# Sigmoid gates stored to DRAM ahead of the scan, and the last branch merge woven by 256 tokens into the output products

## The chip, the cores and the metric

The kernel runs on one core of a Trainium2 chip, as one program on one set of inputs. The metric is the device time of one execution in microseconds (us). The core has a matrix engine (TensorE, PE in the rows, with its weight loads as PEld), a vector engine (VectorE, DVE), a scalar engine (ScalarE, ACT), GpSimd (POOL) and SyncE (SP), which here only issues DMAs. Each engine takes its instructions in the order in which they were placed; an instruction that waits holds up all that stand behind it on that engine.

## The reference

One step of a backbone of one layer, for two groups of tokens: 2048 sample tokens and 128 prompt tokens, 2176 in all, with D = 1024 features.

```python
shift, scale, gate = ada_mod(c, w_ada, b_ada)          # silu(c) @ w_ada + b_ada
xn = rmsnorm(h, ln_g) * (1.0 + scale) + shift
proj = xn @ w_in
qkv, beta, dec, z_a, u_b, v_b, z_b, x_c, z_c, gates = split(proj)
qkv = silu(conv3(qkv))                                  # short centred convolution
o, s_f, s_b = delta_bidir(q, k, v, g, beta, s0_f, s0_b) # A: scan over chunks of 64 tokens, both directions
o_a = rmsnorm(o, o_norm_g) * silu(z_a)
o_b = chunk_sgu(u_b, v_b, ...) * silu(z_b)              # B: spatial gating in chunks of 128
o_c = fourier_mix(x_c, grid) * silu(z_c)                # C: Fourier mixing
pb = [o_a, o_b, o_c] @ w_branch                         # three products 512 -> 1024
merged = sum_n sigmoid(gates[n]) * pb[n]
h = h + gate * (merged @ w_out)
y = rmsnorm(h, final_g)                                 # the final scan states are outputs too
```

## The kernel before

Activations are kept turned (features on partitions) as a pair of fp16 tensors, `xh` and `xl` (high part and remainder, [128, 8, 2176] each). A product of two such pairs is three matmuls (high by high, low by high, high by low). All are recorded at one helper line, L250 (L249 in the changed kernel), so a row's tensors tell what it belongs to. Tokens go in four tiles of 512 and one of 128 (`TBS`).

Weights come by blocks of 128 output columns: `read_w` loads a block in fp32 into `wst` (two buffers), and `converting` makes the pair: ScalarE squares it (L315), a one-column matmul and VectorE make a scale, ScalarE writes the high part (L327), VectorE the low part (L328). `wlist` holds all blocks in the order of use, `getw` takes the next and reads some ahead, `weight_step` does a piece of a conversion between main work.

Main work goes through stages in this order: (1) adaLN, norm and silu(z_a), to 150 us; (2) qkv with its convolution and the decays, to 440; (3) branch B (V, then U and Z_b) and branch C (X_c and Z_c, Fourier steps); (4) `merge(1)`, `merge(2)`, `merge(0)`: per block of 128 output columns and per tile, a gate product of 24 matmuls, its sigmoid on ScalarE into `sg`, a branch product of 12 matmuls, VectorE's product of both (L1739, L1742), and for branches 2 and 0 POOL's sum with what the branches before left (L1743; `mrow`, loaded from and stored to the DRAM tensor `mrg`); (5) the output, `two_tiles` for 256 tokens at a time.

The branch operand is loaded from DRAM (`br`) by `branch_block` (L1689, into `st`, three buffers) and converted into `big` (ScalarE L1699, VectorE L1700). The output uses seven half-size products in place of eight: sums of quarters of w_out are made by `out_w` and staged in DRAM (`tw`), sums of the merged operand by `quarters` within `merge(0)`, staged in `pa`, and both are loaded again by the output. Sample rows for the residual go into `xh`, which nothing reads any more by then (`room`).

Beside stages 3 and 4 runs branch A's delta rule, a generator of small steps (`delta`): first 17 chunk preparations, then an inverse, then the scan of 33 steps and the finished rows. `Pace` interleaves it: each piece of main work adds its estimated microseconds, and for every `QUOTA` = 1.6 (preparation) or `SCAN` = 1.3 (scan) of them one step of the generator is recorded. So the amounts of main work set where on each engine the scan's instructions stand. Preparation lies from 440 to 800 us, the scan's first chain is at 915, its last at 1622. SP's queue carries nearly all loads, in the order of their places.

Of the kernel before, what the change touches and what calls it, by code (L numbers as in the profile page):

```python
# [20 lines left out]
P = 128  # L21
# [11 lines left out]
SCAN = 1.3  # L33
# [4 lines left out]
ADA_D = (6, 7, 12, 13, 14, 15)  # L38
TBS = [(0, 512), (512, 512), (1024, 512), (1536, 512), (2048, 128)]
# [72 lines left out]
def _blocks():  # L112


    parts = [(C_ZA, g) for g in range(4)] + [(C_QKV, i) for i in range(12)] + [(C_V, g) for g in range(4)]
    for pair in ((C_U, C_ZB), (C_XC, C_ZC)):
        parts += [(x_, g) for g in range(4) for x_ in pair]
    return parts + [(C_G + n * D, db) for n in (1, 2, 0) for db in range(KT)]
# [76 lines left out]
def hybrid_flow_kernel(ctx: ExitStack, tc: tile.TileContext, x_prompt, x_sample, state_delta, c, c_ctx, w_ada,  # L195
# [48 lines left out]
    newest, gated_, queued = [None], [None], [False]  # L244

    def behind_gate():
        return tc.issue_after(gated_[0].ins) if queued[0] else ExitStack()
# [37 lines left out]
    turn_of = [None]  # L285
# [10 lines left out]
    def read_w(src, nkt, cols=P, tag="w"):  # L296
        st = sb(wp, [P, nkt, cols], "wst" if cols == P else tag + "st", bufs=2 if cols == P else 1)
        load(st, src.rearrange("p (k c) -> p k c", c=cols))
        return st
# [3 lines left out]
    def converting(w, st, nkt, cols=P, hi=None, lo=None, tag="w", bufs=5, nth=0):  # L303
# [4 lines left out]
        if tag == "v":  # L308
            hi, lo = [t[:, vfilled[0]] for t in v4]
            vfilled[0] += 1  # L310
        w.hi = sb(wpool, [P, nkt, cols], tag + "hi", F16, bufs=bufs) if hi is None else hi
        w.lo = sb(wpool, [P, nkt, cols], tag + "lo", F16, bufs=bufs) if lo is None else lo
        ss = sb(wp, [P, 1], "wss", bufs=4) if nth < KT else bsums[:, 3 + nth:4 + nth]
        with behind_gate():
            w.squared = A.activation(w.lo, st, AF.Square, accum_out=ss)  # L315
# [6 lines left out]
        if isx is None:  # L322
            w.own = inv
        else:
            V.tensor_mul(w.inv, inv, isx)
# [34 lines left out]
    for i, (n_, g) in enumerate(_blocks()):  # L360
        wlist.append((w_blk[i], KT, "z" if n_ == C_ZA else "v" if n_ == C_V else "w", 4))
        if n_ >= C_G:
            n_ = (n_ - C_G) // D
            wlist.append((w_brb[n_, g], 4, "b", 2, n_ * KT + g))
    v4, vfilled = [], [0]
    goal = [0]
# [11 lines left out]
    def begin():  # L378

        i = len(wdone)  # L380
        if i >= goal[0] or (wlist[i][2] == "b" and not bwp):
            return False
# [3 lines left out]
        wsteps.append(converting(wdone[i], wread[i], wlist[i][1], tag=wlist[i][2], bufs=wlist[i][3], nth=(wlist[i] + (0,))[4]))  # L386
# [544 lines left out]
    for ct in range(12):  # L931
        w = getw(1, 2 if ct < 6 else min(4, 15 - ct))
# [24 lines left out]
    wsn = sb(ep, [P, WB], "st", bufs=3).rearrange("p (g q) -> p g q", g=4)  # L957
    with tc.issue_after(behind.ins):
        SY.dma_start(wsn, w_spatial[0].rearrange("g p q -> p g q"))
# [511 lines left out]

    vsD = dram("vs", [4, P, NTOK])
    bs = ExitStack()
# [33 lines left out]
    for t in range(NCH):  # L1507
        ps = bank(ps_mm, [P, 4, P])
        ts = slice(t * P, (t + 1) * P)
        for k in range(KT):  # L1510
            mm(ps, xh[:, k, ts], v4[0][:, :, k, :], k == 0, False)
            mm(ps, xh[:, k, ts], v4[1][:, :, k, :], False, False)
            mm(ps, xl[:, k, ts], v4[0][:, :, k, :], False, k == KT - 1)
        vn = sb(ep, [P, WB], "sg", bufs=4).rearrange("p (i c) -> p i c", i=4)
# [151 lines left out]
    cfs.close()  # L1666


    mD = dram("mrg", [KT, P, NTOK])
    HALVES = [(0, 1024, TBS[0:2]), (1024, 1152, TBS[2:])]  # L1670

    ms_ = ExitStack()
    bwp.append(pool(ms_, "bwp", 1))
    big = pool(ms_, "big", 1)
    mrp = pool(ms_, "mrp", 2)

    o16 = sb(big, [P, 2, 4, NTOK], "big", F16)

    def branch_scale(n, cols):
        ss = sb(ep, [P, 1], "bss2")  # L1680
        V.tensor_reduce(ss, oss[n][:, 0:cols], AX.X, ALU.add)
        V.tensor_copy(bsums[:, n:n + 1], ss)
        return scales(ss, ep, "bsc")

    def branch_block(n, s, t0, tn):

        def loaded(g):
            st = sb(ep, [P, tn], "st", bufs=3)
            SY.dma_start(st, obD[n][g, :, t0:t0 + tn])  # L1689
            return st  # L1690

        sts = [loaded(g) for g in range(3)]
        yield
        for g in range(4):
            if g == 1:
                sts.append(loaded(3))
            st = sts[g]
            with behind_gate():
                A.activation(o16[:, 0, g, t0:t0 + tn], st, AF.Copy, scale=s)  # L1699
            V.scalar_tensor_tensor(o16[:, 1, g, t0:t0 + tn], st, s, o16[:, 0, g, t0:t0 + tn], ALU.mult, ALU.subtract)  # L1700

    def merge(n, first, inv, each=None, halves=HALVES, mid=None, then=None, step=None):

        steps, sinv = iter(()), None
        for db in range(KT):
            gw, bw = getw(2, 2)
            binv = sb(ep, [P, 2], "binv")
            V.tensor_mul(binv[:, 0:1], inv, bw.inv)
            V.tensor_mul(binv[:, 1:2], binv[:, 0:1], sx)
            if each is not None:  # L1710
                each(db)
            if db == KT - 1 and then is not None:
                s_, sinv = branch_scale(*then)
            for h0, hn, tbs in halves:
                mrow = sb(mrp, [P, hn], "mrow")
                if not first:
                    SY.dma_start(mrow, mD[db][:, h0:h0 + hn])
                if each is not None and (n == 0 or db > 3):
                    next(gates, 0)
                for t0, tn in tbs:  # L1720
                    m4 = None
                    if n == 0 and db > 3 and tn == 512:
                        m4 = sb(ep, [P, tn], "st", bufs=3)
                        SY.dma_start(m4, mD[db - 4][:, t0:t0 + tn])
                    if first and db == 0:
                        for tb in TBS[0:2] if t0 == 0 else TBS[TBS.index((t0, tn)) + 1:][:1]:
                            for _ in branch_block(n, s1_, *tb):
                                pass
                    ps = bank(ps_mm, [P, tn])
                    gemm_T(ps, gw, 0, xh[:, :, t0:t0 + tn], xl[:, :, t0:t0 + tn])  # L1730
                    sg = sb(ep, [P, tn], "sg", bufs=4)
                    with tc.high_priority():
                        gated_[0] = A.activation(sg, ps, AF.Sigmoid, scale=gw.inv)  # L1733
                    ps = bank(ps_mm, [P, tn])
                    gemm_T(ps, bw, 0, o16[:, 0, :, t0:t0 + tn], o16[:, 1, :, t0:t0 + tn], nkt=4)
                    mr = mrow[:, t0 - h0:t0 - h0 + tn]
                    if first:
                        with tc.high_priority():
                            V.scalar_tensor_tensor(mr, ps, binv[:, 1:2], sg, ALU.mult, ALU.mult)  # L1739
                    else:  # L1740
                        with tc.high_priority():
                            V.scalar_tensor_tensor(sg, ps, binv[:, 1:2], sg, ALU.mult, ALU.mult)  # L1742
                        G.tensor_tensor(mr, mr, sg, ALU.add)  # L1743
                    if m4 is not None:
                        quarters(db - 4, t0, m4, mr)
                    if n == 0 and t0 == NS and db == KT - 1:
                        as_pair(p16[0][:, db, :], p16[1][:, db, :], mr, ms_s)
                    weight_step()
                    if step is not None:
                        step(db)  # L1750
                    pace.tick(tn * MT)
                    if sinv is not None:
                        for _ in steps:
                            pass
                        steps = branch_block(then[0], s_, t0, tn)
                        next(steps, 0)
                if n:
                    (SY if first else G).dma_start(mD[db][:, h0:h0 + hn], mrow)
                elif db < 4:
                    G.dma_start(mD[db][:, h0:h0 + hn], mrow)  # L1760
                elif h0 and db < KT - 1:
                    G.dma_start(mD[db][:, NS:NTOK], mrow[:, NS - h0:NTOK - h0])
                if mid is not None and db == KT - 1:
                    mid(h0)
        for _ in steps:
            pass
        return sinv

    gateD = dram("gate", [2, D])

    def gate_rows():
        for blk in range(4):
            cs = slice(2 * D + blk * 256, 2 * D + (blk + 1) * 256)
            acc = sb(ep, [P, 512], "sg", bufs=4).rearrange("p (g c) -> p g c", g=2)
            for k0 in range(0, KT, 4):
                st = sb(wp, [P, 4, 256], "wst", bufs=2)
                SY.dma_start(st, w_ada_[k0 * P:(k0 + 4) * P, cs].rearrange("(k p) c -> p k c", p=P))
                yield 1
                ada_sum(acc, st, range(k0, k0 + 4), k0 == 0)
                yield 1  # L1780
# [412 lines left out]
```

## Time and profile before

| | us |
|---|---|
| median of three runs | 2145.65 |
| the runs | 2145.1, 2145.65, 2146.66 |
| span of the profiled execution (first to last instruction) | 2142.8 |
| PE busy in it | 2084.4 |
| mean granted TensorE clock in it | 0.990 of full |

The profile is one execution on the chip. Its own time is known by its span alone; the median of the runs is 2.85 us above that. In rows of groups, `x64` is a count, then come busy us in total, mean ns of one, idle time of the engine before them and what ended it. In rows by window come the length, busy us and count for each engine, the granted clock, the share of the 16 DMA engines' time and GB/s.

### The profile page before, as it was taken

The page shows a single profiled execution, that of the slowest core. Times are in us where ns is not written, and L with a number is a line of the kernel's source. Part 1 is how long each engine was busy: PE and PEld are TensorE (multiplying, and loading weights), DVE is VectorE, ACT ScalarE, POOL GpSimd, SP SyncE. Part 2 cuts the span into 40 slices and gives each one's busy share as a digit, 9 for nine tenths or more (in the row PEclk, how much of TensorE's full clock was granted, in tenths as well). Part 3 has the DMA queues.
Part 4 walks back from the last instruction along what each step waited for, and adds up shares of the span by engine and source line. Part 5 has one row for each costly group of instructions (what it writes and reads, how often), then busy time and mean ns, then how long its engine had stood idle before and what let it go on. Part 6 is the DMA issues. An engine that isn't in the chain of part 4 may idle for free.

```text
span 2142.8 us, 42632 instructions
## 1 busy us (share of the span) xinstructions
PE 2084.4 (97%) x16133; PEld 1197.6 (56%) x16133; DVE 1330.7 (62%) x2945; ACT 1060.6 (49%) x2456; POOL 843.1 (39%) x1089
## 2 busy tenths in 40 slices
PE   8999999999999999999899999999999999999998
PEld 4454444455555677777555556565655444444443
DVE  6656854378777786566655555866665564666245
ACT  5554744465656664445544445665654353443112
POOL 0321332225565554552322233355543234343464
PEclk9999999999999999999999999999999999999999
DMA  9625722177877743444665556867664645456862
GB/s 352 222 78 191 266 103 103 62 222 234 262 226 240 228 143 99 121 132 141 204 182 166 164 160 188 262 211 226 211 198 128 210 169 173 167 197 234 344 221 89
DMA packets 222766, 403.25 MB, mean 188 GB/s; under 512 B 39704, under 2 KB 109616, under 8 KB 219744
## 3 DMA queue, kind: packets, MB, share of 16 engines
q1 hardware_dynamic: 167520, 290.58, 42.5%
q0 software_dynamic: 15216, 65.89, 8.2%
q10 hardware_dynamic: 39824, 44.05, 6.0%
q8 instruction: 127, 2.08, 0.4%
q14 instruction: 79, 0.65, 0.1%
HBM read 258.19 MB, written 142.24 MB: 187 GB/s over the span
## 4 chain that ended last, share of the span: by engine, by line
PE 50%; DVE 8%; DMA 7%; POOL 3%; ACT 3%; issue 3%; SPq 1%; ACTq 0%; POOLq 0%; DVEq 0%
PE b L250 49%; DMA st<-br 3%; POOL E L1115 1%; DMA pa<-pa 1%; DVE XB L1114 1%; POOL st L1466 1%; DVE big L1700 1%; DMA ei<-XB 1%; ACT big L1699 1%; ACT nd L1066 0%; DVE n L1083 0%; POOL ss L1024 0%; DVE XB L1123 0%; DMA br<-st 0%; DMA skn<-kv 0%
## 5 line engine op out<-in xcount | busy, mean ns | idle before, releaser
L250 PE MATMUL b<-xh,whi 128*128 128x512 f16 (+1 forms) x1920 | 650.3, 347 | 2.9 <-DVE sg L1456 1.8
L250 PE MATMUL b<-xl,whi 128*128 128x512 f16 (+1 forms) x1920 | 650.6, 347 | 0.0
L250 PE MATMUL b<-xh,wlo 128*128 128x512 f16 (+1 forms) x1920 | 649.7, 347 | 0.0
L250 PEld LDWEIGHTS <-whi 128*128 128x128 f16 x3856 | 352.4, 98 | 326.1 <-issue 6.9
L250 PEld LDWEIGHTS <-wlo 128*128 128x128 f16 x1928 | 188.6, 98 | 175.6 <-issue 1.2
L250 PE MATMUL b<-big,bhi 128*128 128x512 f16 (+1 forms) x960 | 253.2, 348 | 2.8 <-ACT big L1699 1.5
L250 PE MATMUL b<-big,blo 128*128 128x512 f16 (+1 forms) x480 | 163.4, 347 | 0.0
L1743 POOL TENSOR_TENSOR mrow<-mrow,sg 128x512 f32<-128x512 f32 (+1 forms) x80 | 94.4, 1183 | 129.4 <-DVE sg L1742 98.6
L953 POOL TENSOR_TENSOR cy<-cy,raw 128x545 f32<-128x545 f32 (+1 forms) x48 | 64.5, 1372 | 182.1 <-ACT raw L952 182.1
L250 PEld LDWEIGHTS <-xh 128*128 128x128 f16 x1496 | 117.1, 98 | 28.7 <-issue 1.3
L250 PEld LDWEIGHTS <-bhi 128*128 128x128 f16 x960 | 87.8, 98 | 79.2 <-issue 4.0
L1115 POOL TENSOR_TENSOR E<-E,XB 128x31 f32<-128x31 f32 (+15 forms) x155 | 94.3, 608 | 83.8 <-DVE XB L1114 67.6
L250 PEld LDWEIGHTS <-xl 128*128 128x128 f16 x1068 | 98.1, 98 | 44.8 <-DMA tw<-tw 1.3
L1733 ACT ACTIVATE sg<-b,winv 128x512 f32<-128x512 f32 (+1 forms) x120 | 74.0, 616 | 86.3 <-PE b L250 85.5
L1188 POOL COPY T<-ES 32x256 f16<-32x256 f16 x68 | 30.0, 442 | 182.9 <-DMA ES<-ei 159.6
L250 PE MATMUL b<-whi,xh 128*128 128x128 f16 x544 | 92.8, 219 | 0.0
L250 PE MATMUL b<-whi,xl 128*128 128x128 f16 x544 | 92.8, 219 | 0.0
L250 PE MATMUL b<-wlo,xh 128*128 128x128 f16 x544 | 92.8, 219 | 0.0
L328 DVE SCALAR_TENSOR_TENSOR wlo<-wst,wsc,whi 128x1024 f16<-128x1024 f32 x52 | 69.9, 1345 | 31.8 <-ACT whi L327 30.5
L315 ACT ACTIVATE wlo<-wst 128x1024 f16<-128x1024 f32 x52 | 54.9, 1055 | 53.0 <-DMA wst<-in_w_blk_dram 50.3
L1295 POOL TENSOR_TENSOR skn<-skn,ed 128x512 f32<-128x512 f32 x34 | 37.0, 1089 | 110.5 <-DMA skn<-kv 110.5
L1114 DVE TENSOR_TENSOR XB<-XB,E 128x31 f32<-128x31 f32 (+15 forms) x155 | 54.3, 350 | 42.0 <-POOL E L1115 41.3
(531 smaller groups left out, 4328.9 us busy)
## 6 DMA issues: line engine op xcount, KB each, us to landing
wst<-in_w_blk_dram SPq DMA_DIRECT2D x58, 512.0 KB, 4.5
pa<-pa POOLq DMA_DIRECT2D x16, 896.0 KB, 4.6
qkv<-cy POOLq DMA_DIRECT2D x12, 1089.0 KB, 5.3
st<-br SPq DMA_DIRECT2D x48, 256.0 KB, 3.3
mrow<-mrg SPq DMA_DIRECT2D x16, 576.0 KB, 4.7
pa<-pa SPq DMA_DIRECT2D x5, 1792.0 KB, 17.1
dc<-dec SPq DMA_DIRECT2D x17, 512.0 KB, 4.6
kq<-qkv SPq DMA_DIRECT2D x34, 256.0 KB, 4.3
```

The source lines that it names most:

```text
L250: newest[0] = PE.matmul(out, l, r, start=start, stop=stop, skip_group_check=reopened)
L315: w.squared = A.activation(w.lo, st, AF.Square, accum_out=ss)
L328: w.low = V.scalar_tensor_tensor(w.lo, st, s, w.hi, ALU.mult, ALU.subtract)
L953: G.tensor_tensor(y[:, c0:c1], y[:, c0:c1], raw[:, 1 + c0:1 + c1], ALU.mult)
L1114: V.tensor_tensor(t3, X3[:, 0:k, k:k + 1].to_broadcast([P, k, n_]), E3[:, k:k + 1, k:32].to_broadcast([P, k, n_]), ALU.mult)
L1115: G.tensor_tensor(E3[:, 0:k, k:32], E3[:, 0:k, k:32], t3, ALU.subtract)
L1188: G.tensor_copy(T16[rows(a0, b), :, :, b], ES[0:32, :, 2 * a0 + b, :, wT])
L1295: G.tensor_tensor(h3(kn_), h3(kn_), bc(ed[:, d, t, :], P), ALU.mult)
L1466: G.tensor_tensor(o, sg, src, ALU.mult)
L1699: A.activation(o16[:, 0, g, t0:t0 + tn], st, AF.Copy, scale=s)
L1733: gated_[0] = A.activation(sg, ps, AF.Sigmoid, scale=gw.inv)
L1743: G.tensor_tensor(mr, mr, sg, ALU.add)
```

## The change

- The 24 gate blocks leave the merges. 22 of them (`EARLY`) are done right after qkv, beside the chunk preparation, the last two after branch C; `gate_block` stores the sigmoids to DRAM (`g0`, `g1`, `g2`: 24 blocks of 128 x 2176 fp32, 1.1 MB each). The rows of the adaLN gate (`gate_rows`) are made there too.
- Branches B and C move behind these, beside the scan, whose `SCAN` goes to 1.5. Merges 1 and 2 have no gate product and, but for the scan's end in merge 1, no scan beside them: per tile 12 matmuls, with the gate loaded from DRAM into `sg`. The operand of branch 2 lies in `xh`, the pair of w_out in `xl`; sums of w_out's quarters stay in SBUF (`sums`).
- At block 6 of merge 2 `after_scan` is recorded: the end of w_out, the conversion of branch A's eight weight blocks (tag "c") and the loads of the first units.
- The last merge goes by units of 256 tokens (`merged`, 96 matmuls of 256 columns, then `quarters` in SBUF), each recorded ahead of the products of the pair before it. The merged rows (`mt`) and the output rows (`hh`) have one buffer each, gates, operands and `pa` two.

Its core:

```diff
-SCAN = 1.3
+SCAN = 1.5
+EARLY = 22
...
+    gates = [(C_G + n * D, db) for n in (1, 2, 0) for db in range(KT)]
+    parts = [(C_ZA, g) for g in range(4)] + [(C_QKV, i) for i in range(12)] + gates[:EARLY] + [(C_V, g) for g in range(4)]
...
+    return parts + gates[EARLY:]
...
+    def gate_block(more):
+        n, db = next(gates_of)
+        w = getw(1, more)
+        for t0, tn in TBS:
+            ps = bank(ps_mm, [P, tn])
+            gemm_T(ps, w, 0, xh[:, :, t0:t0 + tn], xl[:, :, t0:t0 + tn])
+            sg = sb(ep, [P, tn], "sg", bufs=4)
+            with tc.high_priority():
+                A.activation(sg, ps, AF.Sigmoid, scale=w.inv)
+            SY.dma_start(gD[n][db][:, t0:t0 + tn], sg)
+            next(gates_rows, 0)
+            pace.tick(tn / 100)
...
+    o16 = {1: sb(big, [P, 2, 4, NTOK], "big", F16), 2: xh.rearrange("p (l k) t -> p l k t", l=2)}
+    whi, wlo = [flat(xl)[:, i * KT * D:(i + 1) * KT * D].rearrange("p (k c) -> p k c", k=KT) for i in range(2)]
...
+    def merge(n, first, inv, each=None, step=None):
...
+            for t0, tn in TBS:
+                gt = sb(ep, [P, tn], "sg", bufs=4)
+                SY.dma_start(gt, gD[n][db][:, t0:t0 + tn])
+                mr = sb(mrp, [P, tn], "mrow")
+                if not first:
+                    SY.dma_start(mr, mD[db][:, t0:t0 + tn])
+                if first and db == 0:
+                    for _ in range(16 if t0 == 0 else 8):
+                        next(own, None)
+                ps = bank(ps_mm, [P, tn])
+                gemm_T(ps, bw, 0, o16[n][:, 0, :, t0:t0 + tn], o16[n][:, 1, :, t0:t0 + tn], nkt=4)
+                with tc.high_priority():
+                    V.scalar_tensor_tensor(mr if first else gt, ps, binv, gt, ALU.mult, ALU.mult)
+                if not first:
+                    G.tensor_tensor(mr, mr, gt, ALU.add)
...
+                (SY if first else G).dma_start(mD[db][:, t0:t0 + tn], mr)
...
+    def load_unit(t0, tn):
+        gt = sb(late_pool[0], [P, 2, 4, tn], "gt", bufs=2)
+        SY.dma_start(gt, gD[0][:, :, t0:t0 + tn].rearrange("(h k) p t -> p h k t", h=2))
+        st = sb(wp, [P, 4, tn], "wst", bufs=2)
+        with tc.issue_after(newest_read[0].ins):
+            SY.dma_start(st, obD[0][:, :, t0:t0 + tn].rearrange("g p t -> p g t"))
+        o = sb(late_pool[0], [P, 2, 4, tn], "o16", F16, bufs=2)
+        as_pair(o[:, 0], o[:, 1], st, held_["s"])
+        return gt, o
...
+    def merged(t0, tn, gt, o):
+        mt = room[:, 6 * D:6 * D + 8 * tn].rearrange("p (h k t) -> p h k t", h=2, k=4)
+        SY.dma_start(mt, mD[:, :, t0:t0 + tn].rearrange("(h k) p t -> p h k t", h=2))
+        for k in range(4):
+            ps = bank(ps_x, [P, 2, tn])
+            for h in range(2):
+                w = cws[4 * h + k]
+                for kk in range(4):
+                    mm3(ps[:, h], (w.hi[:, kk, :], w.lo[:, kk, :]), (o[:, 0, kk, :], o[:, 1, kk, :]), kk == 0, kk == 3)
...
+    ready = [quarters(merged(firsts[0] * P, 2 * P, *held_["first"]))]
...
+    ahead_rows = two_rows(firsts[0])
     for i, t in enumerate(firsts):
+        if i < 7:
+            t0 = firsts[i + 1] * P
+            ready.append(quarters(merged(t0, 2 * P, *load_unit(t0, 2 * P))))
```

How the order changes, at three places.

SP before, at the start of the output (`mrg` is the partial sum, `pa` and `tw` the staged operands, `gate` the adaLN gate, `xh` and `xl` serve as room for the output):

```order
L1724 DMA st_25623<-mrg 128x512
L1921 DMA sg_25558<-gate 128x512
L1965 DMA xh_94<-in_x_prompt_dram 128x512
L1965 DMA xl_95<-pa 128x4x1792
L1965 DMA xl_95<-tw 128x4096 x2
L1965 DMA tw_3065_25690<-tw 128x4096
L1965 DMA xh_94<-in_x_sample_dram 128x1024 x2
L1965 DMA tw_3065_25690<-tw 128x4096
L1965 DMA pa_25703<-pa 128x4x1792
L1965 DMA fg_25689<-in_final_g_dram 128x1024
```

SP after, at the end of merge 2 (`in_w_brb` are branch weights, here of branch A, `g` the stored gates, `br` branch operands; the last row is the first unit's operand; left out are two more weight blocks and merge 2's last gates and partial sums):

```order
L290 DMA wst_24683<-in_w_brb_dram 128x512
L1767 DMA sg_24974<-g_3907 128x512
L1770 DMA mrow_24914<-mrg 128x128
L1945 DMA xh_94<-in_x_sample_dram 128x1024
L290 DMA wst_24700<-in_w_brb_dram 128x512
L1945 DMA xh_94<-in_x_sample_dram 128x1024 x3
L1770 DMA mrow_24936<-mrg 128x512
...
L290 DMA wst_24747<-in_w_brb_dram 128x512
L1770 DMA mrow_25016<-mrg 128x128
L290 DMA wst_24764<-in_w_brb_dram 128x512
L1913 DMA xh_94<-mrg 128x8x256
L1849 DMA wst_24818<-br_3885 128x4x256
```

Before, the row loads stood among loads for the output itself. Now they stand in front of most of branch A's weight blocks and of the first unit's operand, and their target, `xh`, is merge 2's operand.

SP after, at the start of merge 1, from the row before the last two gate stores on (`st<-br` are branch 1's operands, three of which were issued before):

```order
L1767 DMA sg_22695<-g_3906 128x512
L1489 DMA g_3905<-sg_22595 128x512
L1489 DMA g_3905<-sg_22637 128x128
L1767 DMA sg_22762<-g_3906 128x512
L1752 DMA st_22710<-br_3886 128x512
L1752 DMA st_22714<-br_3886 128x512
L1767 DMA sg_22813<-g_3906 128x512
L1752 DMA st_22718<-br_3886 128x512
L290 DMA wst_22747<-in_w_brb_dram 128x512
```

Before, the gates of merge 1 were products of the merge itself; now the stores of the last gates, the loads of the first ones and the operand loads share the queue.

PE before, from `merge(0)`'s last tile to the output's first product (`blo`, `bhi` a branch weight block, `wohi` w_out, `whi` the prompt rows):

```order
L250 MATMUL b_3063_25652<-big_1522_13436,bhi_3018_25213 128x512
L250 LDWEIGHTS bhi_3018_25213
L250 MATMUL b_3063_25652<-big_1522_13436,bhi_3018_25213 128x512
L250 LDWEIGHTS blo_3019_25214
L250 MATMUL b_3063_25652<-big_1522_13436,blo_3019_25214 128x512
L250 LDWEIGHTS whi_3039_25393
L250 MATMUL b_3071_25706<-wohi_2753_23191,whi_3039_25393 128x512
L250 LDWEIGHTS whi_3039_25393
L250 MATMUL b_3071_25706<-wolo_2754_23192,whi_3039_25393 128x512
L250 LDWEIGHTS wlo_3040_25394
```

PE after, from the last tile of merge 2 (in `xh`) to the first product of the last merge; left out are five more matmuls of one column:

```order
L249 LDWEIGHTS blo_2965_24503
L249 MATMUL b_3084_25018<-xh_5_94,blo_2965_24503 128x128
L249 LDWEIGHTS ones16_2_89
L249 MATMUL b_3010_24704<-wscb_3009_24702,ones16_2_89 128x1
...
L249 LDWEIGHTS ones16_2_89
L249 MATMUL b_3042_24794<-bsc0b_3043_24795,ones16_2_89 128x1
L249 LDWEIGHTS ones16_2_89
L249 MATMUL b_3046_24805<-bsums16_3045_24803,ones16_2_89 128x27
L249 LDWEIGHTS whi_2995_24667
L249 MATMUL b_3088_25048<-o16_3049_24820,whi_2995_24667 128x256
```

Before, the product of the prompt rows followed the last merge tile at once. Now the scale matmuls of branch A's weight blocks stand between merge 2 and the first 256-wide product.

More of the change, by code (lines that the diff above doesn't have):

```diff
@@ L1702, in merge @@
[L1702 to L1767, printed above, removed]
@@ L1789, in hybrid_flow_kernel @@
-    gates = gate_rows()
-    s1_, inv_ = branch_scale(1, 20)
-    inv_ = merge(1, True, inv_, then=(2, 20))
-    def finish_delta(db):
-        if db == KT - 1:
-            pace.drain()
-            queued[0] = True
-    early = list(range(KT))
-    def norm_step(db):
-        if db > 1 and early:
-            i = early.pop(0)
-            st = sb(ep, [P, 512], "st", bufs=3)
-            SY.dma_start(st, w_brb[0, i])
-            with tc.issue_after(gated_[0].ins):
-                A.activation(st, st, AF.Square, accum_out=bsums[:, 3 + i:4 + i])
@@ new lines, in hybrid_flow_kernel, with second_block, out_w @@
+    s1_, inv1 = branch_scale(1, 20)
+    s2_, inv2 = branch_scale(2, 20)
+    own, later_ = branch_blocks(1, s1_), branch_blocks(2, s2_)
+    def second_block(db):
+        if db:
+            next(later_, None)
+            next(later_, None)
+    merge(1, True, inv1, step=second_block)
+    for _ in later_:
+        pass
+    tw = sb(big, [P, 4, 4 * D], "big", F16)
+    sums = tw.rearrange("p j (q l k c) -> p j q l k c", q=4, l=2, k=4)
+    q4 = slice(0, 4), slice(4, 8)
+    def out_w():
+        for j in range(4):
+            while j == 3 and not late_pool:
+                yield
+            desk = tw[:, j + 1].bitcast(F32) if j < 3 else sb(late_pool[0], [P, 2 * D], "gt", bufs=2)
+            sts = [desk[:, i * D:(i + 1) * D].rearrange("p (k c) -> p k c", k=KT) for i in range(2)]
+            for st, i in zip(sts, (j, j + 4)):
+                SY.dma_start(st, w_outb[i].rearrange("p (k c) -> p k c", c=P))
@@ L1878, in quarters @@
+    def quarters(mt):
+        pa = sb(er, [P, 4, 2, 7, P], "pa", F16, bufs=2)
+        S = sb(op, [P, 4, 4, P], "sums", bufs=1)
+        x4, x8 = [mt[:, h].rearrange("p k (s c) -> p k s c", s=2) for h in range(2)]
         V.tensor_tensor(S[:, :, 0], x4[:, :, 1], x8[:, :, 1], ALU.add)
```

415 lines of the change are left out of this document (193 added, 222 removed).

## The prediction

> **What bounds the kernel now.** I read the page's head, then busy time by stage, then what TensorE (PE) waited for.
>
> ```profile
> span 2142.8 us, 42632 instructions
> PE 2084.4 (97%) x16133; PEld 1197.6 (56%) x16133; DVE 1330.7 (62%) x2945; ACT 1060.6 (49%) x2456; POOL 843.1 (39%) x1089
> ```
>
> PE is the bound: 58.4 us of the span are idle, 14.5 in the head and 12 in the last stage by the rows below. By stage (length, busy us of PE, PEld, DVE, ACT, POOL, granted clock, DMA share, GB/s):
>
> ```profile
> 0.00:150.00 150.00, 135.47 (x864) 71.67 (x865) 96.59 (x193) 82.34 (x142) 30.48 (x36) 0.98 0.62 228
> 150.00:440.00 290.00, 290.00 (x1671) 142.87 (x1671) 163.81 (x199) 146.73 (x215) 77.37 (x95) 0.99 0.42 145
> 440.00:800.00 360.00, 353.21 (x2774) 217.71 (x2773) 288.52 (x710) 225.29 (x689) 198.49 (x288) 1.00 0.70 223
> 800.00:893.00 93.00, 92.15 (x1254) 76.92 (x1252) 57.60 (x134) 41.63 (x88) 46.71 (x74) 0.98 0.35 97
> 893.00:1080.00 187.00, 168.80 (x2021) 122.92 (x2019) 118.50 (x306) 97.98 (x236) 70.06 (x111) 0.96 0.54 163
> 1080.00:1340.00 260.00, 259.55 (x2375) 155.06 (x2374) 145.42 (x387) 120.11 (x291) 73.63 (x115) 1.00 0.56 170
> 1340.00:1400.00 60.00, 57.62 (x503) 33.88 (x502) 45.22 (x105) 42.05 (x105) 25.21 (x31) 1.00 0.79 252
> 1400.00:1580.00 180.00, 179.62 (x1642) 108.59 (x1640) 114.86 (x288) 105.25 (x303) 90.80 (x115) 1.00 0.70 217
> 1580.00:1650.00 70.00, 68.04 (x521) 38.73 (x520) 38.36 (x100) 32.79 (x99) 25.16 (x23) 0.98 0.49 153
> 1650.00:1993.00 343.00, 341.88 (x1872) 165.75 (x1870) 195.28 (x431) 140.60 (x241) 123.69 (x133) 1.00 0.56 196
> 1993.00:2143.00 150.00, 138.05 (x662) 63.51 (x660) 66.56 (x97) 25.78 (x49) 81.49 (x71) 0.97 0.54 203
> ```
>
> The rows between 440 and 1993 are what the change reorders. Length less busy time sums there to 6.8+0.85+18.2+0.45+2.4+0.4+2.0+1.1 = 32.2 us. Length times (1 − clock) adds 1.9+7.5+1.4 = 10.8. So **43 us** is all that a better order can win; the rest is matmul work. What PE waited for in the worst stage, 893 to 1080 (us in total, times, longest):
>
> ```profile
> PE b L250 <- DMA ES<-ei: 3.5, 2, 2.4
> PE b L250 <- ACT Q L1186: 2.1, 3, 1.0
> PE b L250 <- ACT big L1699: 1.5, 2, 1.1
> ```
>
> Scan steps and branch operands, a few us each: no wait is large.
>
> **The change part by part.** The profiled span is 2142.8; the runs' median, 2145.65, lies 2.85 above it, so I add terms to the span and then 2.85.
>
> Matmul work. The order shows the same gates, branches, scan and products; 384 matmuls of 512 columns become 768 of 256.
>
> ```profile
> L250 PE MATMUL b<-xh,whi 128*128 128x512 f16 x1536 | 582.9, 379 | 2.9 <-DVE sg L1456 1.8 <-DVE sg L1742 1.1
> L250 PE MATMUL b<-whi,xh 128*128 128x128 f16 x544 | 92.8, 219 | 0.0
> ```
>
> (379−219)/384 columns = 0.417 ns a column, so 213 ns for 512 and twice 107 for two of 256. I take **+1** (0 to 2).
>
> The 43 us of idle and half clock is credited in full; what the new order puts in their place is charged.
>
> Chunk prep. It ran beside V, U and Z_b and lost 6.8+0.85 us plus 1.9 of clock. Now it runs beside 22 gate blocks, whose DVE share is smaller: the gate leaves by ScalarE and an SP store, and no product is formed. 22 × 1.1 MB of stores over 22×21.7 = 477 us of gate matmuls (96 of 213 ns and 24 of 53 each) are 51 GB/s, on a stage at share 0.70. The adaLN gate's rows and the qkv stage's shorter read-ahead I cost at nothing: PE was busy for all of row 150:440 with ScalarE at half; without that cover a weight block's landing and conversion would show, some 8 us once. I take **2** (0 to 9.5).
>
> Scan. Its 33 steps ran from inside C to the end of merge 2, and lost little beside gate matmuls (rows 1080 to 1580: 3.25 us). Now V, U, Z_b and C lie beside it, with dependent short steps of their own, as in row 893:1080, which lost 18.2+7.5. Against that, main work per step rises to 1.5/1.3 of what it was. I take **10** (4 to 25).
>
> Start of merge 1. Its 20 branch operand tiles go through three buffers. Three loads stand before the last gate stores in SP's queue, 17 behind (13 of 256 KB, four of 64 KB). The rate when they were last loaded in one go:
>
> ```profile
> 1036.50:1074.50 38.00, 12.79 (x20) 0.96 0.69 213
> DMA to landing us min/median/max: 1.8/3.2/5.4
> ```
>
> The first row is ScalarE's conversion of 20 operand blocks (L1699) in 38 us, 1.9 each; the second is what their loads (L1689) took to land. 13×1.9 + 4×1 = 29 us, against some 17 us of PE work (the first weight block's 48 matmuls of 213 ns and 12 of 53, about 11, and the scan's last chunk): **12** (1 to 20). Before, each tile also had 24 gate matmuls to cover this.
>
> Merges 1 and 2. With no gate matmuls a weight block takes 10.9 us of PE. SP and POOL move per block in merge 2: gate 1.1 MB, partial sum in 1.1, out 1.1, weights 0.25, w_out 0.5: 4.1 MB. POOL's rows:
>
> ```profile
> L1743 POOL TENSOR_TENSOR mrow<-mrow,sg 128x512 f32<-128x512 f32 x64 | 85.1, 1330 | 120.0 <-DVE sg L1742 97.3 <-DVE wsc L277 16.1 <-DVE wscb L264 4.4
> L1743 POOL TENSOR_TENSOR mrow<-mrow,sg 128x128 f32<-128x128 f32 x16 | 9.5, 593 | 9.5 <-DVE wsc L277 8.1 <-DVE sg L1742 1.3
> L1758 POOL DMA_DIRECT2D mrg<-mrow x16 | 9.9, 619 | 4.2 <-POOL mrow L1743 3.9 <-DVE sg L476 0.3
> L1858 POOL TENSOR_TENSOR sums<-pa,sums 128x512 f32<-128x512 f32 x8 | 10.2, 1274 | 0.2
> 0.00:50.00 50.00, 40.74 (x203) 22.18 (x204) 30.51 (x76) 28.12 (x50) 2.54 (x10) 0.97 0.94 366
> 1350.00:1400.00 50.00, 47.62 (x434) 28.50 (x433) 36.17 (x86) 33.43 (x87) 19.92 (x24) 1.00 0.82 262
> 1980.00:1990.00 10.00, 10.00 (x48) 4.53 (x47) 3.40 (x5) 1.99 (x5) 2.86 (x3) 1.00 1.01 422
> ```
>
> Per block POOL has 4×(1.33+0.62) + 0.59+0.62 = 9.0 us, and with w_out's 16 subtractions of 1.27 over six blocks 3.4 more: 12.4, above PE's 10.9, so 6×1.5 = 9. DMA: at the rate that 1350:1400 shows for full engines, 262/0.82 = 320 GB/s, 4.1 MB take 12.8 us, 8×1.9 = 15; at 422, nothing. I take **12** (1 to 29) for both merges.
>
> Between merge 2 and the output: the term that decides. Four loads of sample rows go into xh, which now holds branch 2's operand: they wait for PE's last tile of merge 2. In SP's queue (rows above) four weight blocks of branch A and the first unit's operand stand behind them; the one before them, too, stands behind the first row load. PE's first 256-wide product needs them all, converted. Nothing else is ready for PE: the eight one-column scale matmuls of these blocks stand ahead of it. The price:
>
> ```profile
> wst<-in_w_brb_dram SPq DMA_DIRECT2D x24, 256.0 KB, 3.5
> mrow<-mrg SPq DMA_DIRECT2D x16, 576.0 KB, 4.7
> L315 ACT ACTIVATE blo<-wst 128x512 f16<-128x512 f32 x24 | 14.9, 623 | 2.2 <-DMA wst<-in_w_brb_dram 1.4 <-PE b L250 0.6
> L327 ACT ACTIVATE bhi<-wst,wsc 128x512 f16<-128x512 f32 x24 | 17.2, 717 | 29.5 <-DVE wsc L278 25.4 <-DVE wsc L279 4.0
> L328 DVE SCALAR_TENSOR_TENSOR blo<-wst,wsc,bhi 128x512 f16<-128x512 f32 x24 | 19.3, 805 | 1.8 <-ACT bhi L327 1.5
> L327 ACT ACTIVATE whi<-wst,wsc 128x1024 f16<-128x1024 f32 x52 | 59.3, 1142 | 33.5 <-DVE wsc L278 33.3
> ```
>
> Two buffers, six loads: two rotations of 3.5 to land, 0.62+0.72+0.81 to convert and about 0.75 for the scale between, 6.4 each, then a 512 KB load (4.5, between 3.5 for 256 KB and 4.7 for 576) and 1.14: 18.4 us, and some 2 for the block already loaded, whose scale matmul stands behind the last tile. By bytes: four rows of 512 KB, four or five weight blocks, the rest of merge 2's partial sums in and out, gates, the units: 8.1 MB, 25 us at 320 GB/s, 19 at 422. I take 24 idle (12 to 30, the low end where half is covered). An idle PE comes back at a lower clock: row 893:1080 lost 7.5 us to it with 18 idle; I take 4 (2 to 6). Together **28** (14 to 36). The Trainium skill, page "TensorE: Matmul & The Clock Gate", Part 1, says that after an idle window of about 3.4 us the array runs at half rate until it has been busy about as long; by it the hole costs 1.7 us instead of 4.
>
> Woven output. Eight units of 256 tokens are merged between the products: the unit loads (1 MB of gates, 1 MB of sums, 0.5 MB operands) are issued a pair ahead, but hh, the merged rows and the sums have one buffer. Each product pair of 84 matmuls of 213 ns is 18 us of PE, and a unit 10; 2.5 MB in 28 us are 90 GB/s, so most is hidden: **5** (2 to 20). Staging pa and w_out's sums in DRAM goes; this cost PE 1.15 us at the output's start:
>
> ```profile
> 1990.00:2000.00 10.00, 8.85 (x41) 3.73 (x40) 2.48 (x4) 0.00 (x0) 5.46 (x5) 1.00 1.02 418
> ```
>
> That lies inside the 43.
>
> Sum: 1+2+10+12+12+28+5 = 70, less 43: +27. 2142.8 + 27 + 2.85 = 2172.65, **2172**.
>
> **The rivals.** (B) The loads land early. Without the scan's transfers beside merges and hole, loads take nearer the 1.8 us minimum than 3.2: the start 12→1, merges 12→1, hole 28→18, woven 5→2, 35 less: 2172.65 − 35 = 2138, **faster**. It decides once 27 of the 35 are won, at a median near 2 us. For it: DMA reached 422 GB/s. Against: those transfers were of 1.8 MB each; the queue's order stays, and the 256 KB loads of L1689 took 3.2. The Trainium skill, page "SBUF — State Buffer", "The DMA setup-cost knee", gives 2 us plus bytes over 436 GB/s: an estimate of 2.6 us for 256 KB; the trace's median is longer.
>
> (C) The merges run at DMA's pace. All of merges 1 and 2, with the operands of branches 1 and 2, w_out and hoisted loads, is some 65 MB; at 213/0.69 = 309 GB/s (the branch blocks' row) 210 us against 16×10.9 = 174 of PE: 36 in place of 12, **2196**. For it: the small transfers; against it, merge 1 alone needs just 3.0 MB a block, 9.7 us.
>
> (D) Each woven pair waits on its one buffer, 2.5 us more in eight pairs, 20 for 5: **2187**. For it: the chain through ScalarE, VectorE, POOL and SP per unit; against: 28 us of PE work a pair.
>
> (E) Gains and losses meet: hole at its low end, start and merges half: 2172.65 − 14 − 12 = **2146**, within 0.2% of before (4.3 us, about what a measurement can tell).
>
> **How the numbers follow.** The forecast 0.52, with its own range 2150 to 2190; B 0.17, C 0.13, D 0.11, E 0.07. The range, 2140 to 2202, holds the forecast, E, most of C and D and the upper third of B; it takes in the bounds of the hole and the scan. Faster is B, 0.17; same E, 0.07; slower the rest, 0.76.
>
> **What would show it.** Right: a PE gap of about 20 us between the last 128-wide tile of merge 2 and the first 256-wide product, ended by an operand from br or a weight block; waits on branch operands in merge 1's first tiles; POOL or DMA near full in merge 2. Wrong: a gap under 12 us, PE over 98% busy through both merges, landings of 2 us (B); or the scan beside U, Z_b and C idling PE for over 25 us.

## The result: 4.6% slower, nearly four times the forecast loss

| | before | after |
|---|---|---|
| median, us | 2145.38 | 2247.06 |
| runs, us | 2143.65 to 2146.66 | 2241.58 to 2249.26 |
| span of the profiled execution | 2142.8 | 2246.0 |

The ratio is 1.0462 (95% interval 1.0438 to 1.0486): some 100 us more, where the forecast had 27 and its range ended at 2202. The direction was right, and two terms of the sum came out near their size (matmul work and the hole, as I call the gap of PE between merge 2 and the first 256-wide product); the others were too small.

The head of the page after:

```profile
span 2246.0 us, 43541 instructions
PE 2103.1 (94%) x16517; PEld 1234.2 (55%) x16517; DVE 1326.3 (59%) x2862; ACT 1046.5 (47%) x2380; POOL 841.2 (37%) x1058
```

PE has the same products to do and yet 143 us without work, against 58. By stage, with bounds at the first or last matmul of each (columns as in the prediction): preparation beside gates; scan beside V, U and Z_b; scan beside C; last gates; merge 1; merge 2; the hole; the woven output.

```profile
440.00:920.00 480.00, 462.34 (x2946) 250.72 (x2945) 273.19 (x686) 257.15 (x709) 193.44 (x290) 1.00 0.68 216
920.00:1359.00 439.00, 438.92 (x4048) 265.67 (x4046) 255.07 (x665) 204.74 (x483) 143.18 (x224) 1.00 0.53 164
1359.00:1653.00 294.00, 280.70 (x3922) 229.59 (x3920) 187.34 (x482) 173.79 (x505) 121.47 (x178) 0.97 0.47 143
1653.00:1713.00 60.00, 57.05 (x484) 33.80 (x481) 25.91 (x79) 31.89 (x93) 19.37 (x23) 1.00 0.44 139
1713.00:1823.00 110.00, 97.89 (x516) 46.28 (x515) 61.64 (x137) 39.20 (x82) 2.28 (x2) 0.95 0.86 286
1823.00:1941.00 118.00, 95.36 (x500) 44.57 (x497) 73.05 (x146) 39.42 (x67) 81.96 (x83) 0.97 0.75 248
1941.00:1969.00 28.00, 1.08 (x8) 0.55 (x6) 13.44 (x55) 10.06 (x20) 11.51 (x14) 0.59 0.93 324
1969.00:2233.00 264.00, 248.90 (x1603) 152.04 (x1604) 174.13 (x214) 62.76 (x77) 157.12 (x114) 0.99 0.40 130
```

Idle and half-clock time overlap, so in what follows a stage's **loss** is worked out from the trace's matmuls: the time from each one's start to the next one's, less what is usual for its shape (216 ns for 512 columns, 109 for 256, 56 for 128, the medians of the trace of before).

| stage | loss before | loss after |
|---|---|---|
| to 440 us | 20.9 | 25.8 |
| preparation and inverse, to the scan's first chain | 19.4 | 23.3 |
| scan, and what lay beside it | 28.9 (C, merges 1 and 2) | 27.0 (V, U, Z_b −0.2; C 24.0; last gates 3.2) |
| merge 1 | (in the row above) | 19.8 |
| merge 2 | (in the row above) | 28.8 |
| before the output (merge 0; the hole) | 2.3 | 28.4 |
| output | 0.4 | 19.3 |

The differences sum to 100.5, and some 3 us of tail and matmul work complete the 103.2 by which the spans differ. The head, to 440 us, lost 4.9 more; the reason stays open.

What ended PE's waits after, in merge 1, merge 2, the hole and the woven output (us, times, longest):

```profile
PE b L249 <- ACT big L1743: 6.3, 7, 1.7
PE b L249 <- DVE mrow L1777: 3.5, 2, 3.1
PE b L249 <- DVE sg L1777: 19.2, 13, 4.5
PE b L249 <- DVE wscb L263: 21.1, 5, 5.2
PE b L249 <- ACT o L1743: 5.9, 1, 5.9
PE b L249 <- DVE gt L1921: 8.7, 8, 1.7
```

The first is a branch operand being converted (merge 1). The second and third are VectorE's product that empties a PSUM bank, late in merges 1 and 2. The fourth is a scale on the way through a weight block's conversion, five times in the hole. The fifth, the conversion of the first unit's operand, ends the hole. The last is VectorE emptying a unit's bank.

### The profile page after: what moved, and what is told of

Same layout as the page of the kernel before. It is cut to its first block, busy times and chain, and to the rows that moved or that the text cites. A ratio compares the mean times of both kernels' runs of the same rounds, so it can differ in the third digit from the quotient of the medians.

```text
span 2246.0 us, 43541 instructions
## 1 busy us (share of the span) xinstructions
PE 2103.1 (94%) x16517; PEld 1234.2 (55%) x16517; DVE 1326.3 (59%) x2862; ACT 1046.5 (47%) x2380; POOL 841.2 (37%) x1058
## 5 line engine op out<-in xcount | busy, mean ns | idle before, releaser
L249 PEld LDWEIGHTS <-whi 128*128 128x128 f16 x4416 | 406.1, 98 | 347.6 <-issue 16.4
L249 PEld LDWEIGHTS <-wlo 128*128 128x128 f16 x2208 | 216.4, 98 | 181.8 <-issue 3.7
L249 PEld LDWEIGHTS <-bhi 128*128 128x128 f16 x640 | 60.8, 99 | 99.2 <-issue 42.1
L249 PE MATMUL b<-o,whi 128*128 128x256 f16 (+1 forms) x576 | 93.9, 269 | 15.3 <-DVE gt L1921 8.7
L249 PE MATMUL b<-xh,bhi 128*128 128x512 f16 (+1 forms) x320 | 84.7, 356 | 22.0 <-DVE sg L1777 19.2
L249 PEld LDWEIGHTS <-pa 128*128 128x128 f16 x648 | 62.7, 98 | 73.2 <-DVE pa L1744 4.3
L249 PE MATMUL b<-big,bhi 128*128 128x512 f16 (+1 forms) x320 | 86.6, 357 | 14.8 <-ACT big L1743 6.3
L336 DVE SCALAR_TENSOR_TENSOR wlo<-wst,wsc,whi 128x1024 f16<-128x1024 f32 (+1 forms) x60 | 75.7, 1262 | 40.6 <-ACT whi L335 40.4
L1779 POOL TENSOR_TENSOR mrow<-mrow,sg 128x512 f32<-128x512 f32 (+1 forms) x40 | 50.0, 1258 | 128.3 <-DMA mrow<-mrg 127.1
L249 PE MATMUL b<-big,pa 128*128 128x512 f16 x372 | 85.9, 380 | 2.1 <-DVE pa L1744 1.3
```

The lines of the kernel that those rows point to most:

```text
L249: newest[0] = PE.matmul(out, l, r, start=start, stop=stop, skip_group_check=reopened)
L336: w.low = V.scalar_tensor_tensor(w.lo, st, s, w.hi, ALU.mult, ALU.subtract)
L1779: G.tensor_tensor(mr, mr, gt, ALU.add)
```

## The experiments

Each ran beside the kernel before on its chip; its ratio to that is to be held against the change's 1.0462 [1.0438, 1.0486]. Edits are to the changed kernel and shown shortened. "Off" is the difference of a median to the change's 2247.06, which was measured beside another set of runs of the kernel before; the ratios give up to 6 us less. The intervals of e2, e3, e5, e6, e7, e9, e10 and e13 overlap the change's, so for these the reading rests on the loss of the stage. In stages that an edit leaves alone the loss scatters too, by 2 to 5 us.

**e1: gate stores off SP's queue.** SP waited 181.2 us in 66 places for sigmoids before it could issue their stores:

```profile
SPq L1489 <- ACT sg L1488: 181.2, 66, 10.0
```

```diff
-            SY.dma_start(gD[n][db][:, t0:t0 + tn], sg)
+            A.dma_start(gD[n][db][:, t0:t0 + tn], sg)
```

> Edit: the gate stores beside the chunk preparation are issued from ScalarE, behind the sigmoid that makes them, and not from SP. Between 440 and 900 us the changed kernel loses some 20 us of PE, where the forecast had 2; SP waits there 181 us for sigmoids, with the preparation's loads queued behind. Theory (SP's queue held up by the stores): most of it goes, 10 to 18 us off the whole time, 2230 to 2237. Rival (the preparation's steps come in bursts of three after each gate tile and wait for one another whatever the queue does): the stage stays within 4 us, 2243 to 2251. Rival (ScalarE's issue work delays its own conversions and sigmoids): slower, 2250 or more.

2256.59, ratio 1.0510 [1.0495, 1.0526]: slower. The stage's loss fell from 23.3 to 16.6 (e2 to e5, which leave this stage alone, lie at 18.6 to 21.3, so 2 to 5 us of that are the edit's), but merge 1's rose from 19.8 to 30.6; the reason stays open. SP's 181 us of waiting cost PE little.

**e2 and e3: the hole.** e2 issues the sample rows' loads behind the first units' operands:

```diff
-    ahead_rows = two_rows(firsts[0])
+    ahead_rows = two_rows(firsts[0], newest_unit[0])   # issue_after that load; so for all pairs
```

> Edit: the loads of the sample rows into the buffer of branch 2's operand are issued behind the load of the first units' operands. The prediction's step was that the weight blocks queue behind these loads. If the row loads hold the queue: the hole between merge 2 and the first 256-wide product shrinks from 25 to about 10 us, 2232. Rival (the rotation of two weight buffers, each with a scale matmul that stands behind merge 2's last tile on PE, sets the hole): it shrinks by under 6 us, 2241 to 2248.

2244.47, ratio 1.0454 [1.0435, 1.0473]. The hole's loss went from 28.4 to 26.6: the rival held. The weight blocks did land sooner, at a median of 4.1 us, where the change's hole has 6.1:

```profile
wst<-in_w_brb_dram SPq DMA_DIRECT2D x4, 256.0 KB, 6.1
```

But the chain of conversions got only 2 us shorter by it. e3 lets merge 2 convert branch A's weights between its own:

```diff
+    pairs_ = [(1, g) for g in range(KT)] + [(n_, g) for g in range(KT) for n_ in (2, 0)]   # wlist's order
...
-            bw = getw(1, 2)
+                bw, cw = getw(2, 2)     # in merge 2
+                cws.append(cw)
```

> Edit: branch A's eight weight blocks are read and converted between branch 2's, block by block in merge 2, and no longer all at its end. If the serial conversions at the end of merge 2 are the hole: it goes almost whole (25 to under 5 us); merge 2 carries 0.25 MB and one conversion more per block and may lose a few us: 2222 to 2230. If the row loads alone made it, 10 us or more of it stay: 2235 to 2240.

2237.93, ratio 1.0427 [1.0401, 1.0453], 9 us off. The scale matmuls left the gap, and PE went from merge 2 to the first unit without one. The time itself fell where the expectation had put the row loads, but e2 excludes these: only part of the 28 us was won, since merge 2 lost 37.2 (28.8 in the change), and the first output product now waited for the first unit's operands. PE's longest wait there, and e3's window from the first unit to the first output product, with a loss of 13.8 (the change has 3.2 there):

```profile
PE b L249 <- ACT pa L1744: 8.4, 1, 8.4
```

```profile
1936.00:1974.00 38.00, 25.41 (x252) 20.06 (x251) 18.92 (x34) 4.79 (x7) 23.30 (x25) 0.95 0.91 304
```

So the serial conversions made the hole, and behind them stood the next chain: a unit's products, its sums on POOL, the quarters, the conversion to `pa`.

**e4: the rings of merge 2.** In the change, SP's loads of merge 2 waited for stores to land and for POOL to release gates:

```profile
SPq L1770 <- DMA mrg<-mrow: 31.9, 19, 4.1
SPq L1767 <- POOL mrow L1779: 28.4, 23, 3.0
```

```diff
+    ring.append(pool(r2_, "ring", 8, side="right"))   # scan's pools closed first; blocks 0 to 5
...
+                gt = sb(ring[0], [P, tn], "gm")
+                mr = sb(ring[0], [P, tn], "mrow")
```

> Edit: for blocks 0 to 5 of merge 2, gates and partial sums get eight buffers each and not four. Merge 2 loses 34 us in the changed kernel, where the forecast had 12 for both merges. Theory (a ring: a partial sum's buffer is free only when its store has landed, and SP's later loads wait behind that): the loss of these blocks goes mostly, 18 to 28 us off, 2219 to 2229. Rival (POOL's rate, 12.4 us a block against 10.9, the prediction's price): 9 us of loss stay and the buffers bring under 10 us where a queue was just uneven: 2237 to 2247. Rival (DMA rate): no gain, 2244 to 2250.

2231.20, ratio 1.0392 [1.0370, 1.0414], 16 us off. Merge 2's loss fell from 28.8 to 8.5, as the theory had it; the hole gave back 3.6 of that, and the time, 2231, lies just above the theory's range. Gates and partial sums were widened together, so their shares are not separated. Its window and its waits of the same two kinds:

```profile
1818.00:1915.00 97.00, 89.50 (x494) 43.30 (x492) 68.75 (x138) 38.08 (x64) 78.95 (x83) 1.00 0.83 289
SPq L1769 <- POOL mrow L1781: 10.1, 9, 4.5
SPq L1772 <- DMA mrg<-mrow: 8.0, 7, 3.6
```

POOL, 69% busy in the change's merge 2, is at 81% here, and DMA at 0.83: neither the rate of POOL nor that of DMA had set the 28.8.

**e5 and e6: the start of merge 1.** e5 makes branch 1's operand beside the last gates:

```diff
+            for _ in range(4):
+                next(early_own[0], 0)     # in gate_block: a piece of a load or a conversion
```

> Edit: branch 1's operand blocks are loaded and converted beside the last two gate blocks, and not within merge 1's first weight block. Merge 1 loses 20 us of PE in the changed kernel. Theory (17 operand loads of 1.9 us behind the last gate stores, with only 11 us of products to cover them): the loss falls to 5 or less, 2230 to 2237. Rival (gates and partial sums through four buffers each hold back merge 1 too, as in merge 2): under 6 us gained, 2241 to 2247.

2236.17, ratio 1.0431 [1.0405, 1.0456], 11 us off. Merge 1 lost 7.0 (19.8 in the change), the last gates 6.2 (3.2). e6 undoes one number:

```diff
-SCAN = 1.5
+SCAN = 1.3
```

> Edit: SCAN back at 1.3, so that the scan's steps stand 13% closer together. Theory (the waits beside branch C come from chains of scan and Fourier steps that both are short of main work between them): closer steps wait more, and the scan ends earlier; the C stage loses 24 to 34 us where it lost 22 to 24; 2244 to 2256. Rival (C's own steps wait, whatever the scan does): within 3 us, or a gain as the scan's end moves out of C; 2238 to 2247.

2235.05, ratio 1.0422 [1.0397, 1.0447], 12 us off, more than either side had said. Scan beside V, U, Z_b and C lost 21.3 (5.6+15.7) for 23.8 (−0.2+24.0): closer steps waited more beside V, U and Z_b, and fewer were left for C. The gain is merge 1's, 9.6 for 19.8: the scan's last chain starts at 1612 us instead of 1706 and its finished rows no longer share the queue with merge 1's operands. Both edits relieve one place, by different means.

**e7 and e10: the preparation.**

```diff
+    pace.fine = True          # e7: steps within gate tiles
```

> Edit: the preparation's steps are spread within the gate tiles (after every second k of a product) from the start, and not in bursts after each tile. The stage from 440 us to the scan's first chain loses 19 to 23 us with the change and 19 before it. Theory (bursts: steps of one chunk stand next to each other and wait): 8 to 15 us gained, 2232 to 2239. Rival (the preparation's own chain over its engines is too long for its share of main work): within 4 us, 2243 to 2251.

2253.02, ratio 1.0507 [1.0481, 1.0534]; the stage lost 23.0 (23.3 in the change): bursts are not the cause. Why the time rose above both expectations stays open.

```diff
-QUOTA = 1.6
+QUOTA = 2.0               # e10, with SCAN = 1.3
```

> Edit: QUOTA 2.0 and SCAN 1.3 (against e6_scan13: QUOTA 1.6, SCAN 1.3, 2235): each preparation step gets 25% more main work. Theory (the preparation's PE steps wait since their chain over VectorE, POOL and DMA is longer than the main work between them): the stage to the scan's first chain loses 8 to 12 us where it lost 21; but the scan begins and ends some 80 us later; 2225 to 2240. Rival (these waits belong to single places, as the start and the inverse at the end): 18 us or more stay, 2235 to 2250.

2234.95, ratio 1.0432 [1.0395, 1.0469]: as e6, though the stage's loss fell from 21.1 to 3.2:

```profile
440.00:982.00 542.00, 540.21 (x3400) 291.05 (x3398) 286.21 (x730) 281.33 (x745) 192.11 (x290) 1.00 0.64 202
```

More main work per step takes the preparation's loss away. But the scan began 65 us later, its last chain 80, at 1692, and merge 1 lost 24.6 where e6 lost 9.6. Merge 2 lost 40.6 for 28.2, but its hole 19.6 for 29.6: the two together hardly changed.

**e9 and e13: the woven output.**

```diff
+        for a in range(4):        # e9
+            as_pair(pa[:, a, 0, 3:7], pa[:, a, 1, 3:7], S[:, a], ms_s)
```

> Edit: the 2048-column conversion of the units' sums (VectorE 2.8 us, ScalarE 2.0) is done in four pieces of 512. In the woven output PE waits 8.7 us in 8 places for VectorE to empty one of the two banks that the units use. Theory (the emptying stands behind such long operations): these waits fall to 4 or less, 4 to 8 us off, about 2241. Rival (one buffer for merged rows and output rows paces the pairs): no gain, 2244 to 2251.

2247.29, ratio 1.0477 [1.0449, 1.0505]: no gain. The waits for a unit's bank fell from 8.7 to 5.4 us, and yet the stage lost 24.9 for 19.3.

```diff
-            ps = bank(ps_x, [P, 2, tn])
+            ps = bank(ps_d, [P, 2, tn])     # e13
```

> Edit: the units' 256-wide products use the three banks of another pool in place of two, of which the odd output products use some too. Theory (PE waits in the woven output for one of two banks to be emptied): the 8.7 us of waits on VectorE there fall to 3 or less, 5 to 8 us off the changed kernel, about 2241. Rival (each unit is a chain of VectorE, POOL, ScalarE and SP that paces PE whatever the banks): within 3 us, 2244 to 2250.

2242.88, ratio 1.0443 [1.0428, 1.0459]. The waits for a unit's bank fell from 8.7 to 2.6 us, another took their place, and the stage's loss went from 19.3 to 18.0 only:

```profile
PE b L249 <- DVE st L1986: 5.3, 3, 2.8
PE b L249 <- DVE gt L1921: 2.6, 5, 1.1
```

The banks alone are not it. That the units' chain through VectorE, POOL and ScalarE paces PE fits both runs, but no run removed that chain, so it is argued and not shown.

**e8, e11 and e12: together.** e8 joins e2 to e5. e11 joins e2, e4, e5, e6 and e9, with branch A's weights converted in merge 1. e12 is e11 with QUOTA 2.0 and SCAN 1.15.

> Edit: four edits together: branch A's weights converted within merge 2, the sample rows loaded behind the first units' operands, eight buffers for gates and sums in merge 2's blocks 0 to 5, branch 1's operand made beside the last gates. If the stages' losses are separate, they add: 16 (buffers) + 9 (weights) + 3 (rows) + 12 (operand) = 40 off, 2207. If they are one queue of DMA and POOL work that only moves on to the next stage (as the weights' edit showed: merge 2 lost 8 more and the units 13 of the 28 won): 15 to 25 off, 2222 to 2232. Below 2150, and so beside the kernel before, by none of these.

2217.43, ratio 1.0348 [1.0316, 1.0381], 30 us off by the medians and 24 by the ratios, nearer the second reading. Merge 2 lost 31.9 again, now to weight conversions (11.7 us of PE's waits) and a branch scale (7.1).

> Edit: six edits together: branch A's weights converted between branch 1's in merge 1, sample rows loaded behind the first units' operands, eight buffers in merge 2's blocks 0 to 5, branch 1's operand made beside the last gates, SCAN 1.3, the units' sums in four pieces. If each loss belongs to its stage: merges 1 and 2 lose some 10 us each, the hole 10, the woven output 15: 50 to 60 us off the changed kernel, 2187 to 2197. If queues move the waits on, as in e8_combo: 2205 to 2217. Both above the kernel before: what the gates' matmuls covered there is not to be had back by buffers.

2201.79, ratio 1.0265 [1.0238, 1.0291], 45 us off, between the two readings. Merges 1 and 2 lost 8.6 and 7.6, from the first unit on 42.5.

> Edit: e11_best with QUOTA 2.0 (preparation) and SCAN 1.15 in place of 1.6 and 1.3, so that the preparation gets more main work for each step and the scan still ends near 1610 us. Theory (the preparation's loss is one of pace, 3 us at 2.0 against 17 to 23 at 1.6): 14 us of it go, denser scan steps cost up to 8 more: 2188 to 2197. Rival (loss only moves from the preparation to the scan): 2199 to 2207.

2191.89, ratio 1.0210 [1.0193, 1.0228]: the theory held, with 4.2 lost in the preparation and 22.1 in the scan with C. From its first unit to its first output product:

```profile
1887.00:1923.00 36.00, 22.19 (x228) 18.72 (x228) 23.77 (x33) 5.94 (x8) 20.73 (x19) 0.90 0.76 250
```

The two units take 15.7 us in the change, once their operands are there; here 36. What the hole cost moved to this place. More than half of the change's 100 us could be had back by buffers and pace, and the rest, some 45, not by these; no version here beats the kernel before.

## Why the prediction was right or wrong

**Right: matmul work, direction, the hole's size.** The hole was priced at 28 us, 24 idle and 4 of clock; idle alone measured 28.4, and the clock 1.4 behind it. That the sum came so near was luck: one part was too low, the other too high. The mechanism was half right: the row loads that the prediction put in front cost 2 us (e2); the rotation of two buffers, which it used for the lower price, is what takes the time: five waits of up to 5.2 us, each a load, a square, a scale matmul and the two parts, and only then the next load into that buffer; then 5.9 for the unit's operand. The load was priced at 3.5 us to landing and took 6.1. The scale matmuls stood behind merge 2's last tile on PE, so this chain could not start earlier. The clock term was too big. After the hole:

```profile
1969.30:1972.80 3.50, 2.75 (x13) 1.76 (x14) 1.95 (x2) 0.60 (x1) 0.00 (x0) 0.50 0.47 135
1972.80:1976.30 3.50, 3.50 (x31) 3.02 (x30) 1.41 (x3) 0.00 (x0) 1.19 (x1) 0.92 0.65 202
```

The half clock lasted 3.5 us and a little more; some 14 matmuls took about 105 ns longer each, 1.4 us. That is near the 1.7 that the prediction gave for the rule of the Trainium skill, "TensorE: Matmul & The Clock Gate", Part 1; the 4 was read from row 893:1080, where 13.7 us in two stretches stood at half clock and PE was idle in 3.3 of them.

**Wrong: the credit of 43 us "in full", with 2 for the preparation and 10 for the scan.** This step failed by some 33 us: it made −31 of what measured +2. By matmul starts, preparation and scan with their surroundings had lost 48.3 (19.4+28.9) and now lose 50.3 (23.3+27.0). The waits that were to go came back elsewhere, at two places. The scan still stands beside C's Fourier steps: it lost 20.2 there before (915 to 1080) and 24.0 after, while V, U and Z_b beside it lost nothing. More main work per step, for which the prediction took 10 and not the 18.2+7.5 of row 893:1080, hardly moves this: the scan with V, U, Z_b and C loses 17.8 to 22.7 in e6, e10, e11 and e12, at SCAN 1.3 and 1.15, for 23.8 at 1.5. And the preparation was priced as if gates were the better neighbour, since VectorE is less busy beside them. Before and after, from 440 to 790:

```profile
440.00:790.00 350.00, 346.46 (x2692) 211.66 (x2691) 280.52 (x687) 219.60 (x663) 190.62 (x274) 1.00 0.72 227
440.00:790.00 350.00, 334.81 (x2187) 186.09 (x2185) 220.08 (x551) 203.40 (x598) 147.68 (x213) 1.00 0.74 238
```

At the same pace of steps the loss is 4.4 us beside V, U and Z_b (C's first products from 740 on), and 19.1 beside the gates. Of the 19.1, the stores on SP's queue make 2 to 5 us (e1) and bursts nothing (e7); more main work per step takes all but 0.7 away (e10, 440 to 867). Why gates are the worse neighbour stays open. The other 15.0 of the 19.4 before fell from 790 on, beside C's Fourier steps and the inverse; after, 4.2 fall there. Of the 76 us between forecast and profile, about 33 lie in this step, 25 in the merges, 14 in the output, 7 in head and tail; the hole and the matmul work give 2 back.

**Wrong: merges 1 and 2, 12 for the start and 12 for the rest; measured 19.8 + 28.8 = 48.6.** Merge 1: operand loads and the scan's end in one queue (e5, e6), the mechanism named, the size low; it came to the upper bound, 20. Merge 2: the price was by rates, POOL's 12.4 us a block and DMA's 12.8, and rival C too was one of rate. What bound it was latency through four buffers (e4). A partial sum is loaded (3.2 us to landing in this stage), waits for its product, is added (1.27), stored (issue 0.56, landing 3.9), and only then is its buffer free for the load four tiles on; gates go round likewise, in the same in-order queue. These pieces alone are 9 us, before any wait for the product, and four tiles of PE work are 10.4: a loop with hardly any slack. This sum is an estimate; that more buffers end the loss is what e4 shows. The rows behind this:

```profile
mrg<-mrow POOLq DMA_DIRECT2D x23, 256.0 KB, 3.9
mrow<-mrg SPq DMA_DIRECT2D x21, 256.0 KB, 3.2
```

With eight buffers the same work ran with 8.5 us of loss (e4).

**Wrong: the woven output, 5 for a measured 19.3.** Rival D had 20, by its one-buffer chain; the size fits, the cause is open (e9, e13).

**The rivals.** B's condition, a median near 2 us, did not come. The branch operands' loads (L1752) took longer than before's 3.2:

```profile
DMA to landing us min/median/max: 2.0/4.1/5.7
```

The 422 GB/s that B and the merges' price point to came with transfers of 0.5 to 1.8 MB (`xh`, `pa`), not of 1.8 each. C named the right stage and the wrong limit. E was far off. The range, up to 2202, had taken each stage's case by itself; here several came at once.

## What to carry to other kernels

When work that covered a chain of small steps is exchanged, don't credit the old waits: price what the chain loses beside its new neighbour and at its pace (main work per step). Here the same pace lost 4.4 us beside one neighbour and 19.1 beside another. For a load, compute and store loop, add up one buffer's way round (load landing, wait, compute, store landing) and divide by the number of buffers, before comparing rates; and where several weight blocks must be converted at a stage's end, count the serial rounds, since each may include a matmul that stands behind the stage's last tile. After filling such a hole, look for the next chain at the same place before counting the gain.

## What the runs showed that was not expected

SP stood 181 us in wait for sigmoids in the preparation, and moving those stores to ScalarE made the kernel slower, not faster (ratio 1.0510 against 1.0462): a queue's waiting time by itself says little. And two rearrangements of the preparation and the scan (e6, e10) moved the loss of merge 1, which comes hundreds of microseconds later, from 19.8 to 9.6 and 24.6 us; e6 also moved the scan's last chain from 1706 to 1612.
